# Half of the gate projections and the merge gate moved behind the scan, as pairs of column tiles computed with Strassen's seven block products

## The chip, the cores and the metric

The kernel runs on one core of one Trainium2 chip. The metric is device time in microseconds (us). The kernel before takes 2431.65 us, the median of three runs (2431.22 to 2434.09).

The engines are named as the profile names them: PE (TensorE matmul), PEld (its weight loads), DVE (VectorE), ACT (ScalarE), POOL (GpSimd) and SP (SyncE, which here issues every DMA, in the order of its queue). Each engine runs its own instructions in order. Semaphores join the engines.

## The reference, cut to what matters

Two layers of this are computed, over 1024 tokens of width 1024, in float32, and one final RMSNorm:

```python
h = rms_norm(x, norm_g) * (1.0 + scale) + shift
proj = h @ w_in                       # 1024 x 1024 times 1024 x 8320
pool_u, pool_g, q, k, v, ret_g, rw, rw_g, gate_logits = split(proj)
o_pool = causal_pool_mixer(pool_u) * silu(pool_g)
o_ret  = retention(q, k, v) * silu(ret_g)
o_rwkv = rwkv7_time_mix(rw) * silu(rw_g)      # a scan over the tokens
y = einsum('btnw,nwd->btnd', stack(o_pool, o_ret, o_rwkv), w_branch)
gates = sigmoid(gate_logits.reshape(B, T, 3, 1024))
x = x + gate * (sum(gates * y, axis=2) @ w_out)
```

The columns of `gate_logits` (24 tiles of 128, "gates" below) and of `rw_g` (4 tiles, "wg" below) depend on h alone and are needed only when the branches are merged. They can be computed at any time before that.

## The kernel before, in words

**Matmuls.** Everything is kept transposed: features on the 128 partitions, tokens along the free axis in two halves h of 512. A float32 value is split into two float32r parts (hi by a cast on ACT, lo by a subtraction on POOL or DVE: `split`, L561). A product of two such values is three matmuls: hi·hi, hi·lo, lo·hi (`mm1`, L548). One *item* is one 128-wide column tile of a weight matrix: for h @ w_in it is 2 halves of the tokens x 8 tiles of 128 features x 3 = 48 matmuls of 128x512 (`in_tile2`, L1431), which sum in two of the three PSUM buffers `acc` (L558). Its weights are loaded and split one item ahead by `wprep` (L512), through buffers `wr` (raw), `wh` and `wl` (hi, lo), three of each.

**The scan.** RWKV's scan is done in chunks of 64 tokens for four pairs of heads, one pair after the other (`rwkv_task`, L783). For each pair there is a preparation for either half of the tokens (`prepare`, L800: DVE and ACT work that makes AR, BK and Z; it begins with six `lw` matmuls), then transposes and scores (`scores`, L889: tiles bt, BKt, g, G), then the inversion of triangular blocks (`invert`, L928: 30 dependent steps `tm` on DVE; the matmuls `av`, then `m`), and then 16 chunk steps (L1004 to L1052), each a chain PE, DVE, PE, DVE, PE, DVE through the tiles two, xst, ch, Z, ch and S. After 8 steps comes a layer norm (L1055) and one transposition `yt` with the output `wob` (L1058).

**The order.** Independent chains (the lanes norm, post, rwkv, mix, ada; L310) are Python generators. Each yields how long it wants to wait by a cost model of its own; after every matmul of an item, `pump` (L415) advances the lanes that are due. So the matmuls of the items lie between the dependent matmuls of the scan and cover the time in which PE would wait. A scheduler in the tile layer then orders the instructions of each engine, and may pull an independent instruction forward. `plan_layer` (L471) decides which item comes next: the items of the next pair of heads (k, r, v), those of the retention of this pair (rq, rk, rv, rg) and of the pooling (pu, pg) when they may be used, and otherwise a gate ("pre") or, late, a wg ("late"). There is always an item to give. When the last pair of heads is nearly done, ("merge",) ends this stage; what is left of gates and wg follows, mixed with the branch projections `br`, and then the output projection `out`.

With this order 20 gates and 3 wg of the first layer and 16 gates and 3 wg of the second lie beside the scan; 4 and 8 gates and one wg each come after it. An early gate is stored to DRAM (`gd`, L1155) and loaded again for the merge (L1499). A wg is multiplied into the scan's output in DRAM (`od`: loaded, multiplied, stored; L1145 to L1150). `load_o` (L1471) loads these outputs for the branch projections through the four buffers `mo` and splits them (oz, oy, oG).

Of the kernel before, what the change touches and what calls it, by code (L numbers as in the profile page):

```python
# [9 lines left out]
F32 = mybir.dt.float32  # L10
# [7 lines left out]
P = 128  # L18
D = 1024
# [47 lines left out]
def GT(n, *ds):  # L67
    return [("gate", n, d) for d in ds]


def BR(n, *ds):
    return [("br", n, d) for d in ds]
# [17 lines left out]
for _c in (16, 20):  # L90
    ADA.append((_c, [_c + _i for _i in range(4)], _n))
    _n += 8
FIRST = [("lora",), ("k", 0), ("r", 0)]


@with_exitstack
def trunk_kernel(ctx, tc, xT, cvec, pos, vecs, consts, w_ada, w_all, pool_w, lora_w, out):
# [15 lines left out]
    def gtile(s):  # L113
        return gp.tile([P, 32 * P + 8], F32, tag="G", name=nm(s))
# [153 lines left out]
    def rope_tables():  # L268
        yield 15000
        MAGIC = 12582912.0  # L270
        TWO_PI = 2.0 * math.pi
        cw, left = [], TWO_PI
        for _ in range(3):
            e = 2.0 ** (math.frexp(left)[1] - 8)
            cw.append(math.floor(left / e) * e)
            left -= cw[-1]
        cw.append(left)
        PI_F = 3.1415925
        for h in range(2):
            s = slice(h * HF, (h + 1) * HF)  # L280
            pi = t_ri("posi", I32)
            tc.keep_in_program_order(nc.sync.dma_start(out=pi, in_=pos[:, s].to_broadcast([P, HF])))
            ang = t_ri("ang")
            nc.vector.tensor_copy(ang, pi)
            nc.vector.tensor_scalar_mul(ang, ang, cs("freq"))
            n = t_ri("nrot")
# [6 lines left out]
            m = t_ri("over")  # L293
# [103 lines left out]
    def until(t):  # L397
        return max(0.0, t - clock[0])
# [72 lines left out]
    def plan_layer(l):  # L471
        yield from [("lora",)] + RW(0)
        pools = deque(PL(i) for i in range(4))
        pre = deque(GT(0, *range(8)) + GT(1, 0, 1, 4, 5, 6, 7) + GT(2, 2, 3, 4, 5, 6, 7, 0, 1) + GT(1, 2, 3))
        late = deque([("wg", 0), ("wg", 1), ("wg", 2)])
        done = 0
        while done < 4 or prog.get((l, 3), 0) < 13 or pools or halves[l] < 15:
            if done < 4 and prog.get((l, done), -1) >= 0:
                done += 1
                if done < 4:  # L480
                    yield from RW(done)
                yield from RT(done - 1)
            elif pools and 4 - len(pools) <= done and len(lanes["mix"]) < 2:
                yield from pools.popleft()
            elif pre or late:
                q = late if late and (done == 4 and prog.get((l, 3), -1) >= 0 or not pre) else pre
                it = q.popleft()
                early[l].add(it)
                yield it
            elif pools:  # L490
                yield from pools.popleft()
            elif done < 4:
                done += 1
                if done < 4:
                    yield from RW(done)
                yield from RT(done - 1)
            else:
                break
        yield ("merge",)
        seq = GT(1, 2, 3) + BR(0, 0, 2, 4, 6) + [("wg", 0), ("wg", 1)]  # L500
        seq += GT(1, 0, 1) + BR(1, 0) + [("wg", 2), ("wg", 3)] + BR(1, 2) + GT(1, 4, 5) + BR(1, 4)
        seq += GT(1, 6, 7) + BR(1, 6)
        seq += GT(2, 0, 1) + BR(2, 0) + GT(2, 2, 3) + BR(2, 2) + GT(2, 4, 5, 6, 7) + BR(2, 4, 6)
        yield from [it for it in seq if it not in early[l]]
        for part in range(2 + (l + 1 == L)):
            yield from [("out", d, part) for d in out_order(l, part)]

# [2 lines left out]
    wready = deque()  # L510

    def wprep(big=False):  # L512
        for l, it in planner:
            if it != ("merge",):
                break
            wready.append((it, None))
        else:
# [128 lines left out]
    def affine_lo(x, r, eng):  # L646
        eng.tensor_tensor(r[1], x, r[0].bitcast(F32), op=ALU.subtract)
# [135 lines left out]
    def rwkv_task(l, hp, kT, rT, vp, lt, lw):  # L783
# [507 lines left out]
    with tc.manual_schedule(engines={ET.PE, ET.DVE, ET.Activation, ET.Pool}):  # L1291
# [114 lines left out]
        mms(1, 6)  # L1406
        mms(1, 7)
    seen[0] = len(nc.cur_bb.bb.instructions)
    L_ = (0, {}, {}, [])
    L_[3].extend(lora_load(0))  # L1410
    for i in range(3):
# [8 lines left out]
    for l in range(L):  # L1420
# [35 lines left out]
        while late_ada:  # L1456
            task = add("ada", ada(*late_ada.pop(0), t_lt))
            if len(gate_ada) < 2:
                gate_ada.append(task)
        merged = None  # L1460
        gates = {}

# [28 lines left out]
        def prefetch():  # L1491
            for j in range(min(2, len(brs))):
                n, d0 = brs[j]
                for d in (d0, d0 + 1):
                    if ("gate", n, d) in early[l] and (n, d, 0) not in gates:
# [220 lines left out]
```

## Time and profile before

| | |
|---|---|
| median of three runs | 2431.65 us |
| the profiled execution's own time | 2434.12 us |
| its span, first to last instruction | 2432.3 us |
| around the span | 1.8 us |
| mean granted clock of TensorE | 0.991 |
| DMA | 219.46 MB, mean 90 GB/s |

Read it by stage: up to about 80 us the first norm and the first three items; then, for each of four pairs of heads, some 200 us of preparation, inversion and chunk steps with items between them (first layer up to 914 us, second from 1263 to 2090 us); then what is left of the gates with the branches, and the output projection. Busy shares are averages over these stages.

### The profile page before, as it was taken

To read this page: it belongs to the slowest core of one execution; us is meant where nothing else is said; L and a number is where in the kernel's file an instruction comes from. 1 tells how busy PE (TensorE), PEld (TensorE's weight loads), DVE (VectorE), ACT (ScalarE), POOL (GpSimd) and SP (SyncE) were. 2 spreads that over 40 slices of the span, in tenths; PEclk is the share of its full clock that TensorE was granted. 3 is DMA by queue.
4 is the path that set the end of the run, shared out by engine and by line. 5 is a ranking of instruction groups with operands and counts; after the bars stand their busy time and mean duration, and the time that the engine had idled before them with its cause. 6 is when DMAs were issued, how large, how long until landed. Compare 5 with 4: busy or idle time off the path is not lost. (4 is left out here: it accounts for less than half of the span.)

```text
span 2432.3 us, 34706 instructions
## 1 busy us (share of the span) xinstructions
PE 2347.7 (97%) x13312; PEld 1921.0 (79%) x13312; DVE 1310.9 (54%) x2564; ACT 800.1 (33%) x1481; POOL 819.3 (34%) x729
## 2 busy tenths in 40 slices
PE   5989999999999999999999999999999999999998
PEld 4768878877877888877877887787788788788888
DVE  7664476467368642457455646836745764221344
ACT  5542242233333223122443324323323323312243
POOL 4321332233231424462442232323323332546241
PEclk9999999999999999999999999999999999999999
DMA  7132112111123225656431211211211222552242
GB/s 252 49 101 79 40 36 80 41 38 62 62 64 93 84 71 179 195 182 221 132 118 41 69 40 36 88 35 49 67 53 38 69 79 68 167 156 91 83 126 79
DMA packets 121910, 219.46 MB, mean 90 GB/s; under 512 B 13840, under 2 KB 17168, under 8 KB 121744
## 3 DMA queue, kind: packets, MB, share of 16 engines
q1 hardware_dynamic: 121744, 217.24, 28.7%
q8 instruction: 104, 1.70, 0.3%
q14 instruction: 62, 0.51, 0.1%
HBM read 172.36 MB, written 44.83 MB: 89 GB/s over the span
## 5 line engine op out<-in xcount | busy, mean ns | idle before, releaser
L563 POOL TENSOR_TENSOR wl<-wr,wh 128x512 fp32r<-128x512 f32 x342 | 456.0, 1334 | 1089.1 <-ACT wh L562 1004.1
L445 PE MATMUL acc<-hlo,wh 128*128 128x512 f32 x2000 | 807.7, 404 | 0.0
L445 PE MATMUL acc<-hhi,wh 128*128 128x512 f32 x2000 | 806.5, 403 | 0.0
L445 PE MATMUL acc<-hhi,wl 128*128 128x512 f32 x2000 | 804.5, 402 | 1.5 <-POOL r L1074 1.5
L445 PEld LDWEIGHTS acc<-hhi,wl 128*128 128x128 f32 x2000 | 378.4, 189 | 68.9 <-POOL r L1074 2.0
L445 PEld LDWEIGHTS acc<-hhi,wh 128*128 128x128 f32 x2000 | 378.4, 189 | 67.8 <-issue 1.1
L445 PEld LDWEIGHTS acc<-hlo,wh 128*128 128x128 f32 x2000 | 378.6, 189 | 67.2 <-issue 2.7
L562 ACT CAST wh<-wr 128x512 fp32r<-128x512 f32 x342 | 211.7, 619 | 654.3 <-PE acc L445 418.7
L1036 DVE SCALAR_TENSOR_TENSOR S<-ch,pc,SP 64x64 f32<-64x64 f32 x256 | 72.5, 283 | 107.6 <-PE ch L445 105.2
L1024 DVE TENSOR_TENSOR xst<-two,MT 64x128 f32<-64x128 f32 x128 | 37.6, 293 | 146.2 <-PE two L445 127.0
L1012 ACT ACTIVATE SP<-S,pc 128x128 f32<-128x128 f32 x128 | 51.4, 402 | 179.8 <-DVE S L1036 171.0
L1540 DVE SCALAR_TENSOR_TENSOR mrg<-gs,acc 128x512 f32<-128x512 f32 x32 | 21.9, 687 | 118.8 <-PE acc L445 118.7
L1542 DVE SCALAR_TENSOR_TENSOR gs<-gs,acc 128x512 f32<-128x512 f32 x64 | 43.6, 683 | 78.0 <-PE acc L445 76.0
L445 PE MATMUL acc<-oz,wh 128*128 128x512 f32 x256 | 81.3, 397 | 1.8 <-DVE gs L1542 1.5
L949 DVE TENSOR_TENSOR two<-two,tm 64x30 f32<-64x30 f32 (+14 forms) x240 | 79.0, 329 | 7.4
L445 PE MATMUL acc<-oy,wh 128*128 128x512 f32 x256 | 80.7, 395 | 1.2 <-DVE mrg L1540 0.8
L943 DVE TENSOR_TENSOR tm<-MT,two 64x30 f32<-64x30 f32 (+14 forms) x240 | 76.4, 318 | 8.2 <-ACT two L936 1.1
L445 PE MATMUL acc<-oG,wh 128*128 128x512 f32 x256 | 79.7, 393 | 0.6 <-DVE gs L1542 0.6
L1031 DVE COPY Z<-ch 64x128 f32<-64x128 f32 x128 | 36.0, 282 | 78.5 <-PE ch L445 77.9
L235 DVE SCALAR_TENSOR_TENSOR ada_acc<-wada,cact,ada_acc 128x512 f32<-128x512 f32 (+1 forms) x70 | 58.8, 840 | 31.5 <-DMA wada<-in_w_ada 30.7
L575 POOL TENSOR_TENSOR vr<-vr,fixed 128x8 f32<-128x8 f32 (+1 forms) x32 | 43.7, 1366 | 85.9 <-DVE vr L574 56.8
L445 PE MATMUL acc<-mhi,wh 128*128 128x512 f32 (+1 forms) x176 | 65.4, 371 | 0.7 <-DVE xres L1588 0.7
(298 smaller groups left out, 3899.6 us busy)
## 6 DMA issues: line engine op xcount, KB each, us to landing
wr<-in_w_all SPq DMA_DIRECT2D x364, 256.0 KB, 2.7
gd<-gsg SPq DMA_DIRECT2D x72, 256.0 KB, 2.0
gs<-gd SPq DMA_DIRECT2D x72, 256.0 KB, 3.4
wada<-in_w_ada SPq DMA_DIRECT2D x70, 256.0 KB, 2.9
ol<-od SPq DMA_DIRECT2D x64, 256.0 KB, 3.0
ringG<-in_w_ada SPq DMA_DIRECT2D x26, 256.0 KB, 4.9
x<-in_xT SPq DMA_DIRECT2D x16, 256.0 KB, 4.9
od<-po SPq DMA_DIRECT2D x16, 256.0 KB, 2.0
```

The lines of the kernel that those rows point to most:

```text
L235: nc.vector.scalar_tensor_tensor(part if kt < NKT - 1 else acc, w, cact[:, kt : kt + 1], part, op0=ALU.mult, op1=ALU.add)
L445: return nc.tensor.matmul(out, lhsT=lhsT, rhs=rhs, start=start, stop=stop, **kw)
L562: nc.scalar.copy(hi, src)
L563: eng.tensor_tensor(lo, src, hi.bitcast(F32), op=ALU.subtract)
L575: nc.gpsimd.tensor_tensor(x, x, mhalf.to_broadcast([P, x.free_size()]), op=ALU.pow)
L943: nc.vector.tensor_tensor(pr, L3[:, i + 1 :, i : i + 1].to_broadcast([64, n, i]), M3[:, i : i + 1, 0:i].to_broadcast([64, n, i]), op=ALU.mult,
L949: nc.vector.tensor_tensor(M3[:, i + 1 :, 0:i], M3[:, i + 1 :, 0:i], pr, op=ALU.add)
L1012: nc.scalar.activation(SP, S, AF.Copy, scale=pcc)
L1024: nc.vector.tensor_tensor(xst[0:64, :], cy[64:128, 0:P], AV[:, c * P : (c + 1) * P], op=ALU.add)
L1031: nc.vector.tensor_copy(Z[0:64, c, :], ch[0:64, 0:P])
L1036: nc.vector.scalar_tensor_tensor(Sn[rw, rw], ch[rw, P + 64 * hd : P + 64 * hd + 64], pc[rw, c : c + 1], SP[rw, rw], op0=ALU.mult, op1=ALU.add,
L1542: nc.vector.scalar_tensor_tensor(s, s, 1.0, ps, op0=ALU.add, op1=ALU.mult)
```

## The change

In each layer at most 12 of the 24 gates now lie beside the scan: `EARLY` caps their number at 4, 6, 8, 10 and 12 as pairs of heads get ready, and where no other item may be given either, the plan yields ("idle",): the planner moves its clock on to the next due lane and gives PE nothing. After the merge come two gates as before. The other ten gates and the four wg are seven pairs of column tiles. A pair is a product of 256 x 1024 weights with 1024 x 1024 activations: 2 x 2 blocks (each block of weights 128 columns x 512 features, each block of h 512 features x 512 tokens). It is computed by seven block products with sums taken before and after (Winograd's order of them) and not by eight. The branch projections then follow without a break.

For this, h is stored to DRAM when it is made (16 tiles of 256 KB per layer) and loaded again (16 tiles, `traw`); four combinations of its blocks are formed on DVE and split (`form`); for each pair of column tiles four weight tiles are loaded (`wraw`), four sums are formed on DVE and seven operands are split (`wforms`); a product is 12 matmuls (`prod`). Between the products ACT copies three partial sums and DVE adds two. Also, the first scores of a pair of heads now wait in the planner for Z, and the tables of the rotary positions are built in other buffers.

In the built program 7752 matmuls write 128x512 sums of items, 168 fewer than the 7920 before (7 pairs x 12 x 2 layers). DVE has 132, ACT 116, POOL 58 and SP 112 instructions more. 96 gate halves are stored to DRAM and loaded again, not 72.

```diff
+EARLY = (4, 6, 8, 10, 12)
...
     xd = [dp.tile([8, 2, P, HF], F32, name=f"xd{l}") for l in range(1)]
+    hd = [dp.tile([8, 2, P, HF], F32, name=f"hd{l}") for l in range(L)]
...
-        pre = deque(GT(0, *range(8)) + GT(1, 0, 1, 4, 5, 6, 7) + GT(2, 2, 3, 4, 5, 6, 7, 0, 1) + GT(1, 2, 3))
-        late = deque([("wg", 0), ("wg", 1), ("wg", 2)])
+        gates = deque(GT(0, *range(8)) + GT(1, *range(8)) + GT(2, *range(8)))
...
-            elif pre or late:
-                q = late if late and (done == 4 and prog.get((l, 3), -1) >= 0 or not pre) else pre
-                it = q.popleft()
-                early[l].add(it)
-                yield it
...
+            elif 24 - len(gates) < EARLY[done]:
+                yield gates.popleft()
             else:
-                break
+                yield ("idle",)
         yield ("merge",)
...
+        for _ in range(2 + len(gates) % 2):
+            yield gates.popleft()
+        rest = list(gates) + [("wg", i) for i in range(4)]
+        yield ("forms", [(rest[i], rest[i + 1]) for i in range(0, len(rest), 2)])
+        for n in range(3):
+            yield from BR(n, 0, 2, 4, 6)
...
+            nc.sync.dma_start(out=hd[l][kt, late], in_=xs[kt])
...
-            yield until(whole[h] + 1000)
+            yield max(until(whole[h] + 1000), wait(Z))
...
+            if ws is None:
+                clock[0] = max(clock[0], min((due[k] for k in names if lanes[k]), default=0.0))
+                pump()
+                wprep()
+                continue
...
+        def form(f, room):
+            sub = lambda o, x, y: nc.vector.tensor_tensor(o, x, y, op=ALU.subtract)
+            for kt in range(4):
+                b11, b12, b21, b22 = raws[4 * kt : 4 * kt + 4]
+                if f == 0:
+                    sub(b11, b12, b11)
+                elif f == 1:
+                    sub(b12, b22, b12)
+                    sub(b22, b22, b11)
+                elif f == 3:
+                    sub(b21, b21, b22)
+                x = (b11, b22, b12, b21)[f]
+                hi, lo = room(kt)
+                split(x, hi, lo, nc.vector if kt % 2 else nc.gpsimd)
+                TT[f].append((hi, lo))
+                yield 1300
...
+            for i in range(len(pairs)):
+                a11, a21, a22, a12 = nxt
+                yield wsplit(a11)
+                s1 = comb(a21, a22, ALU.add)
+                yield wsplit(s1)
+                s2 = comb(s1, a11, ALU.subtract)
+                yield wsplit(s2)
+                yield wsplit(a12)
+                yield wsplit(comb(a11, a21, ALU.subtract))
+                yield wsplit(comb(a12, s2, ALU.subtract))
+                if i + 1 < len(pairs):
+                    nxt = loads(i + 1)
+                yield wsplit(a22)
...
+        for p, (ia, ib) in enumerate(pairs):
+            last = p + 1 == len(pairs)
+            ca = acc_ps()
+            prod(ca, b11, True)
+            cd, cb = acc_ps(), acc_ps()
+            nc.scalar.copy(cb, ca)
...
+            prod(cd, TT[0], True)
+            s5 = t_cc("s5")
+            nc.scalar.copy(s5, cd)
...
+            prod(cb, TT[1], False)
+            s2 = t_cc("s2")
+            nc.scalar.copy(s2, cb)
+            prod(ca, b21, False)
+            evac(ia, ca, 0)
...
+            prod(cb, TT[2], False)
+            nc.vector.tensor_tensor(s5, cb, s5, op=ALU.add)
+            evac(ib, s5, 1)
+            prod(cd, b22, False)
+            nc.vector.tensor_tensor(s2, cd, s2, op=ALU.add)
+            evac(ia, s2, 1)
...
+            prod(cb, TT[3], False)
+            evac(ib, cb, 0)
```

More of the change, by code (lines that the diff above doesn't have):

```diff
@@ L292, in rope_tables @@
                 yield 6000
-            m = t_ri("over")
+            m = mi("over")
             nc.vector.tensor_scalar_add(n, ang, math.pi / 2)
@@ L512, in wprep @@
     def wprep(big=False):
+        if wready and wready[-1][0][0] == "forms":
+            return
         for l, it in planner:
-            if it != ("merge",):
+            if it[0] not in ("merge", "idle", "forms"):
                 break
             wready.append((it, None))
+            if it[0] != "merge":
+                return
         else:
@@ L1408, in trunk_kernel @@
     seen[0] = len(nc.cur_bb.bb.instructions)
+    for h in range(2):
+        for kt in range(8):
+            nc.sync.dma_start(out=hd[0][kt, h], in_=xin[h][kt])
     L_ = (0, {}, {}, [])
@@ L1459, in trunk_kernel, with load_h @@
                 gate_ada.append(task)
+        TT = [[] for _ in range(4)]
+        raws = []
+        def load_h(kt, tile_):
+            for k, h in ((kt, 0), (kt, 1), (kt + 4, 0), (kt + 4, 1)):
+                x = (next(tile_) if kt == 2 else tile_)("traw")
+                nc.sync.dma_start(out=x, in_=hd[l][k, h])
+                raws.append(x)
+        def form(f, room):
[14 more added lines that the diff above has]
+                yield 1300
@@ new lines, in trunk_kernel, with roomy, room @@
+        for kt in range(4):
+            load_h(kt, mi if kt < 2 else t_ri if kt == 3 else iter((t_vp, t_vp, t_cs, t_cs)))
+        def roomy(n):
+            t = []
+            def room(kt):
+                if n == 2:
+                    if kt == 0:
+                        t.append(gtile("T"))
+                    o = 2 * kt * HF
+                elif n < 2:
+                    if kt % 2 == 0:
+                        t.append(r8("T"))
+                    o = kt % 2 * D
+                else:
+                    return hb("thi"), hb("tlo")
+                return t[-1][:, o : o + HF].bitcast(F32R), t[-1][:, o + HF : o + D].bitcast(F32R)
+            return room
@@ new lines, in trunk_kernel, with loads @@
+        tasks = [add("norm", form(f, roomy(f))) for f in range(3)]
+        while wready[0][0][0] != "forms":
+            it, ws = wready.popleft()
+            wprep()
+            for h, ps in enumerate(in_tile2(ws)):
+                evac(it, ps, h)
+        pairs = wready.popleft()[0][1]
+        tasks.append(add("norm", form(3, roomy(3))))
+        drain("post")
+        def loads(i):
+            a, b = pairs[i]
+            r = []
+            for it, j in ((a, 0), (b, 0), (b, 1), (a, 1)):
+                r.append((mi if i % 2 else t_rk)("wraw"))
+                nc.sync.dma_start(out=r[-1], in_=w_all[l, ITEMS.index(it), j])
+            return r
@@ new lines, in trunk_kernel, with prod @@
+        ready_w = deque()
+        source = wforms()
+        def prod(ps, b, first):
+            while len(ready_w) < 3:
+                w = next(source, None)
+                if w is None:
+                    break
+                ready_w.append(w)
+            if len(ready_w) == 1:
+                wprep()
+            w = ready_w.popleft()
+            settle()
+            if not first:
+                clock[0] = max(clock[0], ready.get(ps.tensor.name, 0.0))
+            for k in range(4):
+                ks = slice(k * P, (k + 1) * P)
+                for j, (x, y) in enumerate(((w[0], b[k][0]), (w[0], b[k][1]), (w[1], b[k][0]))):
+                    mmul(ps, x[:, ks], y, start=first and k + j == 0, stop=k == 3 and j == 2, skip_group_check=True)
+                    pump()
@@ L1494, in prefetch @@
                 for d in (d0, d0 + 1):
-                    if ("gate", n, d) in early[l] and (n, d, 0) not in gates:
+                    if (n, d, 0) not in gates:
                         if j and len(gs_free) < 7:
```

39 lines of the change are left out of this document (24 added, 15 removed).

## The prediction, made before the run

> **What bounds the kernel now.** I read the page first, then the waits of PE, then windows by stage, then the timeline of one pair of heads. The page's first part and three of its groups:
>
> ```profile
> span 2432.3 us, 34706 instructions
> PE 2347.7 (97%) x13312; PEld 1921.0 (79%) x13312; DVE 1310.9 (54%) x2564; ACT 800.1 (33%) x1481; POOL 819.3 (34%) x729
> ...
> L563 POOL TENSOR_TENSOR wl<-wr,wh 128x512 fp32r<-128x512 f32 x342 | 456.0, 1334 | 1089.1 <-ACT wh L562 1004.1
> ...
> L562 ACT CAST wh<-wr 128x512 fp32r<-128x512 f32 x342 | 211.7, 619 | 654.3 <-PE acc L445 418.7
> ...
> ol<-od SPq DMA_DIRECT2D x64, 256.0 KB, 3.0
> ```
>
> PE is busy for 97% of the span and no other engine for more than 54%. By stage (us, busy time and count of PE, granted clock, DMA share, GB/s) it is the same: a pair of heads in the scan, the last pair of the first layer, and the stage behind it.
>
> ```profile
> 306.00:508.00 202.00, 197.07 (x1214) 0.99 0.17 51
> 707.00:914.00 207.00, 200.21 (x1249) 0.98 0.28 85
> 914.00:1145.00 231.00, 228.47 (x1034) 1.00 0.61 192
> ```
>
> PE works without a break beside the scan (197 of 202 us) and behind it (228 of 231). What it waits for is little (us in total, times, longest):
>
> ```profile
> PE bt L451 <- ACT Z L872: 10.1, 6, 3.1
> PE two L445 <- ACT aT L809: 7.5, 1, 7.5
> ...
> PE acc L445 <- DVE gs L1542: 2.5, 4, 1.5
> ```
>
> So the time is PE's work, and an edit is worth the matmuls that it takes away, less each new wait of PE. The question is how many new waits come: before, the gates were the cover of the scan.
>
> **Term 1, the matmuls taken away.** Dense 128x512 matmuls of items, the first and the last of nine that follow each other:
>
> ```profile
> 470.37 0.39 PE L445 MATMUL acc<-hhi,wl 128*128 128x512 f32 x1
> 472.19 0.40 PE L445 MATMUL acc<-hlo,wh 128*128 128x512 f32 x1
> ```
>
> Eight steps take 1.82 us: 0.2275 us from start to start (the busy time of one, 0.39 us, overlaps with the next). 168 fewer are 168 x 0.2275 = **-38.2 us**. All of it is on the path, since PE is.
>
> **Term 2, cover taken from the scan.** From the built order: beside the scan the items have 281 matmuls less in the first layer and 219 less in the second. If the scan can't go faster than before, they leave 500 x 0.2275 = 113.8 us of holes; if it can, none. So I need the floor of each stretch of the scan without cover. First the preparation of the second pair of heads (last `lw` to first `av`), and behind it the inversion, to the first `m`:
>
> ```profile
> 328.43 0.39 PE L445 MATMUL lw<-lt,lw 64*128 64x512 f32 x1
> 331.73 0.78 PE L451 MATMUL bt<-cst,BK 128*128 128x128 f32 x4 [2.25 <-ACT Z L872]
> 351.35 0.69 DVE L858 TENSOR_TENSOR BK<-aT,Lc 128x512 f32<-128x512 f32 x1
> ...
> 367.68 0.68 DVE L907 TENSOR_TENSOR G<-two,cst 128x512 f32<-128x512 f32 x1
> 370.58 0.62 PE L445 MATMUL av<-Z,G 64*64 64x64 f32 x7
> 406.19 2.07 DVE L952 STREAM_TRANSPOSE MT<-two 32x1024 f32<-32x1024 f32 x1
> 420.63 1.19 PE L445 MATMUL m<-MT,G 32*32 32x32 f32 x32
> ```
>
> BK is whole at 352.04, 23.6 us behind `lw`; G is whole only at 368.36, because PE has items between its transposes and scores. Without them that part is 8 transposes, 16 pairs of scores and four evictions of 0.68 us: I estimate 7 us from these rows, so the floor of the stretch is 30.6 us. It took 42.15. The order now has 59 item matmuls there, not 98 (8.9 us less), and some 3 us of small matmuls of the retention go into the chunk steps. PE's own work falls to about 27 us (42.15 - 3.3 of waits - 8.9 - 3): a wait of 3.6 us, as much as now. In the other pairs that lose cover here (third and fourth of the first layer, third and fourth of the second) 90 to 114 become 52 to 61; the same sum gives waits of 0 to 8 us. Over the five I take **+13 us** more than now; ends 0 and 40.
>
> The inversion took 50.05 us from `av` to `m`, but T13 was there at 408.26: floor 37.7 us. The order takes 30 matmuls (6.8 us) and some small ones away: about 40 us of PE. No new wait.
>
> One chunk step:
>
> ```profile
> 473.86 0.38 PE L445 MATMUL two<-S,AR 128*128 128x128 f32 x2
> 474.35 0.29 DVE L1024 TENSOR_TENSOR xst<-two,MT 64x128 f32<-64x128 f32 x1 [0.93 <-PE two L445]
> 475.00 0.39 PE L445 MATMUL ch<-xst,G 128*65 128x64 f32 x4
> 475.44 0.28 DVE L1031 COPY Z<-ch 64x128 f32<-64x128 f32 x1 [0.79 <-PE ch L445]
> 476.22 0.38 PE L445 MATMUL ch<-Z,BKt 128*128 128x128 f32 x2
> 476.64 0.58 DVE L1036 SCALAR_TENSOR_TENSOR S<-ch,pc,SP 64x64 f32<-64x64 f32 x2 [0.92 <-PE ch L445]
> ```
>
> From a PE start to DVE's start are 0.49, 0.44 and 0.42 us, DVE's work is 0.29, 0.28 and 0.58, and each way back about 0.06: a floor of 2.7 us. Twelve item matmuls (2.73 us) and the step's own hide that with room. The order keeps 12 in most steps, but 9 in the last pair of each layer (2.05 us and some 0.7 of its own): at the floor, and there the scheduler has put subtractions of `form` (0.69 us each, as the BK row) among DVE's steps. With the stretch from `m` to the first step, where 36 become 5 in the first layer and 21 in the second, I take 8 us per last pair, **+16 us**; ends 0 and 40.
>
> **Term 3, from the scan to the products.** The last chunk step of the first layer, and the layer norm behind it:
>
> ```profile
> 913.75 0.40 PE L445 MATMUL two<-Z,G 128*65 128x64 f32 x4
> ...
> 921.51 1.04 POOL L709 TENSOR_TENSOR yc<-yc,vr 128x512 f32<-128x512 f32 x1
> ```
>
> 8.8 us pass until yc can be transposed. Now 47 matmuls lie between in the second layer; then 13 and 15 (3.0 to 3.4 us) stand ahead of `yt` in PE's queue, and the products behind it: a wait of 5 us. DVE then has wob, one subtraction and one sum (0.7 us each) ahead of the second product's weights, which need a cast (0.62) and a subtraction on POOL (1.33): 3 us more. **+16 us** in two layers; ends 4 and 24.
>
> **Term 4, from the products to the branches.** The last product ends with a wg. Its way from the sum to DRAM, as it is now:
>
> ```profile
> 921.86 0.60 ACT L1116 ACTIVATE wsg<-acc 128x512 f32<-128x512 f32 x1 [4.33 <-DMA od<-ol]
> 922.49 0.69 DVE L1117 SCALAR_TENSOR_TENSOR wsg<-wsg,acc 128x512 f32<-128x512 f32 x1 [0.77 <-ACT wsg L1116]
> 923.22 0.75 DVE L1149 SCALAR_TENSOR_TENSOR ol<-ol,vec,wsg 128x512 f32<-128x512 f32 x1
> ...
> 924.00 0.32 SPq L1150 DMA_DIRECT2D od<-ol  x1
> ```
>
> 2.2 us. In the new order this store stands on SP ahead of three of the four loads that the first branch matmuls need, so these wait behind the last product. One load lands after 3.0 us, a cast takes 0.62, and POOL's four subtractions 1.33 each: the last operand is there about 10.7 us behind the last product, and PE has 24 matmuls (5.5 us) to do with the first three. A wait of 8 us where nothing else lies between, **+16 us** in two layers; ends 0 and 24.
>
> **Term 5, the clock.** The stall of 2.25 us ahead of `bt`, the stretch behind it, and the same in the last pair (PE busy, granted clock):
>
> ```profile
> 329.00:332.00 3.00, 0.75 (x4) 1.00 0.01 3
> 332.00:335.50 3.50, 3.50 (x13) 0.52 0.00 0
> 335.50:340.00 4.50, 4.50 (x33) 1.00 0.25 62
> ...
> 728.00:735.00 7.00, 6.08 (x21) 0.51 0.62 187
> ```
>
> After such a stall PE runs at half clock for 3.4 to 6.8 us and so loses another 1.7 to 3.4. Terms 2 to 4 hold some nine stalls of over 2 us (three preparations, four of term 3, two of term 4): 9 x 1.7 = **+15 us**; ends 0 and 40. The Trainium skill (TensorE: Matmul & The Clock Gate, Part 1) has the clock fall only after an idle window of about 3.4 us; by that rule only the four long stalls of terms 3 and 4 count, +7 and not +15. The trace disagrees in the size of the gap: 2.25 us were enough.
>
> **Term 6, what runs denser.** In a pair POOL splits seven operands, 7 x 1.33 = 9.3 us, beside 84 x 0.2275 = 19.1 us of PE; ACT makes seven casts, three copies and four evacuations of some 0.6 us, 8.7; DVE six sums of 0.69 and its share of the adaLN work. They hide beside PE; without that cover POOL's part is 1.33 us of each product. The branches follow without gates between them; their wait now is 2.5 us (DVE gs). I take +4 us for both; ends 0 and 25. The 64 DMAs for h and 48 for gates are issued by SP beside the scan, at a DMA share of 0.17 to 0.28, and at 0.61 behind it: nothing, with one end in what they would delay (in the 25). The new wait for Z, ahead of `bt`, may save the 10.1 us of that row and moves what is queued behind `bt` on PE; I take nothing, ends -15 and 0.
>
> **Sum** against the profiled execution's own 2434.1 us (span 2432.3 and 1.8 around it): -38.2 + 13 + 16 + 16 + 16 + 15 + 4 = +41.8, 2475.9 us. That execution is 2.5 us above the median of the runs (2431.65), so the forecast for the median is **2474 us**.
>
> **The rivals.**
> - *The scan closes up and the edges are covered* (faster). The scheduler has pulled later items, forms and loads forward already; if the five preparations wait no more than now and the two edges cost half, the new waits come to some 17 us with little half clock, -38 + 17: 2411 us. It decides when terms 2 to 6 stay under 38.2 us. For it: `m` stood 12.4 us behind T13, so the scan has slack. Against it: DVE's 23.6 us to BK.
> - *The holes stay* (slower by much). The scan keeps its length since its order is the planner's and DVE's chain the bound: -38.2 + 113.8 + 47 (terms 3 to 5) = +123, 2554 us. Against it: floors of 30.6, 37.7 and 2.7 us against 42.15, 50.05 and some 3.9 now.
> - *The short stalls don't touch the clock.* Only the four longest (5 us in term 3, 8 us in term 4) cost a half clock of 1.7 us each, 7 us and not 15: 2465 us. For it: over a whole pair of heads, with its waits, the mean clock is still 0.99; against it the window at 332. This is what the rule of the Trainium skill (TensorE: Matmul & The Clock Gate) would make of it.
> - *It cancels*: waits of about 38 us, within 5 us of the time before.
>
> **How the numbers follow.** The forecast has 0.40, the clock rival 0.15, the holes 0.15, other slower mixtures of the ends 0.06; faster 0.18; no difference 0.06. A measurement of this kernel can tell about 0.2% (5 us) from no change: faster 0.18, same 0.06, slower 0.76. The range must reach into the first two rivals to leave no more than 2 in 10 out: 2408 to 2550 us. Among the slower cases alone the forecast's own range is 2450 to 2505.
>
> **What would show it.** Term 1: 168 item matmuls fewer at the same 0.228 us, and windows in the products in which PE is busy throughout. Term 2: gaps of PE ahead of `bt`, `g` and `av` in the preparations, released by DVE BK or G; a pair of heads that takes about 180 us, not 200, is the scan closing up. Term 3: PE yt waiting for yc, then a product waiting for POOL wl. Term 4: PE acc waiting for oz behind the last product. Term 5: more windows at a clock of 0.5. I am wrong if pairs of heads still take 200 us with long gaps, if the products wait for their weights, or if the edges show no gap.

## The result, and the profile after

The changed kernel takes **2487.41 us** (median of four runs, 2484.20 to 2492.41), the kernel before on the same chip 2432.87 us: ratio 1.0224, 95% interval 1.0203 to 1.0245, slower. The forecast was 2474 us. The profiled execution took 2484.2 us, its span 2482.4, at a mean granted clock of 0.974 (before 0.991).

The first lines of the changed kernel's page:

```profile
span 2482.4 us, 35126 instructions
PE 2348.1 (95%) x13144; PEld 1914.6 (77%) x13144; DVE 1433.0 (58%) x2696; ACT 866.1 (35%) x1597; POOL 913.0 (37%) x787
```

PE has 168 matmuls less and the same busy time, 2348.1 against 2347.7 us. So 38 us of work went away and the rest of PE's work became as much longer; the idle time came on top.

Where it happened is seen best in windows by stage (us, PE's busy time and count, granted clock, DMA share, GB/s): the scan and what lies behind it, for both layers. Before:

```profile
92.00:913.00 821.00, 795.37 (x4869) 0.99 0.21 65
913.00:1291.00 378.00, 373.22 (x1694) 1.00 0.53 166
1291.00:2090.00 799.00, 779.78 (x4836) 1.00 0.19 58
2090.00:2426.00 336.00, 333.17 (x1663) 1.00 0.38 116
```

After:

```profile
92.00:867.50 775.50, 742.84 (x4620) 0.98 0.21 65
867.50:1318.00 450.50, 425.83 (x1861) 0.97 0.55 174
1318.00:2083.50 765.50, 742.24 (x4619) 0.98 0.18 57
2083.50:2476.00 392.50, 372.14 (x1799) 0.97 0.43 139
```

Both scans together went from 1620 to 1541 us, 79 less; the 500 matmuls taken out of them are 113.8 us, so 35 us were lost there. Behind the scans it went from 714 to 843, 129 more; the 332 matmuls that came there on balance are 75.5 us, so 53 were lost. PE's idle time (length less busy) rose by 11 us in the scans (44.9 to 55.9) and by 37 behind them (7.6 to 45.0). The clock went from 0.99 and 1.00 to 0.97 and 0.98 everywhere: in the trace's record of it PE worked 34.4 us at half clock before and 97.0 after. In these stretches dense 128x512 matmuls start every 0.43 us (four steps from 886.33 to 888.04) and not every 0.2275, so about half of that time is lost, by estimate 17.2 against 48.5 us. The balance: -38.2 of matmuls, +50 of idle time, +31 of half clock, +43; the span grew by 50.1. About 7 us of slower work I can't place; by the same sums it lies in the scans, where of the 35 us lost 11 are idle time, 14 are half clock (PE worked 24.4 us at it there before, 51.7 after) and 10 are left.

The pairs of heads did close up. The second and the last pair of the first layer, and the products behind it:

```profile
311.00:499.00 188.00, 182.10 (x1169) 1.00 0.15 47
682.00:867.50 185.50, 171.78 (x1070) 0.94 0.33 104
867.50:1042.00 174.50, 152.48 (x662) 0.93 0.60 191
```

188 and 185.5 us stand against 202 and 207 before. In the second layer the third and the last pair went from 200 and 215 us to 194 and 185. PE is idle for 22 us of the 174.5 in the products. What PE waits for in the changed kernel (us, times, longest):

```profile
PE yt L453 <- POOL yc L706: 20.7, 4, 8.5
...
PE acc L447 <- ACT oz L558: 12.9, 2, 6.9
PE acc L447 <- ACT gsg L1151: 9.5, 3, 4.8
PE bt L453 <- ACT Z L869: 9.0, 5, 4.1
...
PE acc L447 <- DVE s L1601: 4.4, 3, 2.1
```

`yt` is the edge from the scan to the products, `oz` the edge from the products to the branches: both stops were forecast, and both are there in both layers. The rows behind the first one (start, us, engine, operation, the idle time before it):

```profile
866.31 2.99 POOL L559 TENSOR_TENSOR T<-traw,T 128x512 fp32r<-128x512 f32 x2 [0.41 <-ACT T L558]
...
869.40 3.45 POOL L559 TENSOR_TENSOR T<-traw,T 128x512 fp32r<-128x512 f32 x2
...
869.88 1.27 DVE L693 TENSOR_SCALAR mn<-mn 128x8 f32<-128x8 f32 x1
...
872.82 1.04 POOL L696 TENSOR_TENSOR yc<-y,mn 128x512 f32<-128x512 f32 x1
...
873.82 2.48 POOL L559 TENSOR_TENSOR T<-traw,T 128x512 fp32r<-128x512 f32 x2
...
875.27 1.06 DVE L570 TENSOR_SCALAR vr<-vr 128x8 f32<-128x8 f32 x1
876.41 1.63 POOL L571 TENSOR_TENSOR vr<-vr,fixed 128x8 f32<-128x8 f32 x1
878.12 1.04 POOL L706 TENSOR_TENSOR yc<-yc,vr 128x512 f32<-128x512 f32 x1
879.21 0.72 PEld L453 LDWEIGHTS yt<-cst,yc 128*128 128x128 f32 x4 [8.89 <-POOL yc L706]
```

POOL splits the T operands of the products ahead of, and in the middle of, the layer norm: between y and yc it has four splits in its queue, and so the way from the last chunk step to yc takes 11.8 us (867.32 to 879.16), not the 8.8 of before. 1.7 us of it are yc's wait in POOL's queue: mn is done at 871.15 and yc begins at 872.82. Two small operations on DVE, `mn` and `vr`, are slow besides: they take 1.27 and 1.06 us and took 0.17 each in the kernel before:

```profile
915.20 0.17 DVE L696 TENSOR_SCALAR mn<-mn 128x8 f32<-128x8 f32 x1
...
919.54 0.17 DVE L574 TENSOR_SCALAR vr<-vr 128x8 f32<-128x8 f32 x1
```

`vr` begins while POOL splits and ends with the split (876.33 and 876.30); at the second layer's edge it takes 1.06 us again and ends at 2092.34, the split at 2092.31. That POOL's splits hold DVE here is inferred from these ends; no run varied it.

### The profile page after: what moved, and what is told of

Read it like the earlier page. It is cut to its first block, busy times and chain, and to the rows that moved or that the text cites. A ratio compares the mean times of both kernels' runs of the same rounds, so it can differ in the third digit from the quotient of the medians.

```text
span 2482.4 us, 35126 instructions
## 1 busy us (share of the span) xinstructions
PE 2348.1 (95%) x13144; PEld 1914.6 (77%) x13144; DVE 1433.0 (58%) x2696; ACT 866.1 (35%) x1597; POOL 913.0 (37%) x787
## 5 line engine op out<-in xcount | busy, mean ns | idle before, releaser
L559 POOL TENSOR_TENSOR wl<-wr,wh 128x512 fp32r<-128x512 f32 x282 | 377.4, 1339 | 866.2 <-ACT wh L558 821.7
L447 PE MATMUL acc<-hhi,wh 128*128 128x512 f32 x1688 | 684.5, 405 | 10.4 <-ACT gsg L1151 9.5
L447 PE MATMUL acc<-hhi,wl 128*128 128x512 f32 x1688 | 686.2, 406 | 0.0
L447 PE MATMUL acc<-hlo,wh 128*128 128x512 f32 x1688 | 683.5, 405 | 0.0
L447 PEld LDWEIGHTS acc<-hhi,wh 128*128 128x128 f32 x1688 | 321.0, 190 | 69.9 <-ACT gsg L1151 10.9
L447 PEld LDWEIGHTS acc<-hlo,wh 128*128 128x128 f32 x1688 | 321.0, 190 | 58.0 <-issue 2.2
L447 PEld LDWEIGHTS acc<-hhi,wl 128*128 128x128 f32 x1688 | 321.0, 190 | 55.3 <-issue 0.7
L559 POOL TENSOR_TENSOR wl<-wsum,wh 128x512 fp32r<-128x512 f32 x56 | 78.6, 1405 | 114.2 <-ACT wh L558 111.2
L447 PE MATMUL acc<-T,wh 128*128 128x512 f32 x336 | 111.7, 415 | 2.7 <-ACT wh L558 2.7
L447 PE MATMUL acc<-oz,wh 128*128 128x512 f32 x256 | 85.3, 415 | 14.1 <-ACT oz L558 12.9
L447 PEld LDWEIGHTS acc<-T,wh 128*128 128x128 f32 x336 | 66.6, 200 | 18.1 <-ACT wh L558 3.1
```

The source lines that it names most:

```text
L447: return nc.tensor.matmul(out, lhsT=lhsT, rhs=rhs, start=start, stop=stop, **kw)
L559: eng.tensor_tensor(lo, src, hi.bitcast(F32), op=ALU.subtract)
```

## The experiments

Medians in us; before, on the same chips, was 2432.56 to 2433.3. All compute the whole reference; e4 adds matmuls that nobody reads.

| run | what it is | median | ratio (95%) |
|---|---|---|---|
| changed kernel | cap 4 to 12, 14 pairs | 2487.41 | 1.0224 (1.0203 to 1.0245) |
| e1_plain | cap 4 to 12, no pairs | 2484.05 | 1.0212 (1.0197 to 1.0227) |
| e2_wg_earlier | pairs, wg in the middle | 2491.87 | 1.0242 (1.0219 to 1.0265) |
| e3_two_more | 12 pairs, four gates ahead | 2478.84 | 1.0193 (1.0174 to 1.0213) |
| e4_keep_busy | pairs, unread matmuls at the edges | 2489.64 | 1.0225 (1.0205 to 1.0246) |
| e5_plain_cap22 | cap 22, no pairs | 2456.48 | 1.0096 (1.0081 to 1.0111) |
| e6_pairs_cap22 | cap 22, 5 pairs | 2461.80 | 1.0124 (1.0107 to 1.0142) |
| e7_pairs_mid | cap 6 to 17, 8 pairs | 2466.83 | 1.0143 (1.0115 to 1.0170) |
| e8_plain_o_first | e5, branch operands early | 2441.00 | 1.0033 (1.0023 to 1.0042) |
| e9_both_edges | changed kernel, both edges moved | 2463.43 | 1.0123 (1.0108 to 1.0139) |
| e10_mid_edges | e7, both edges moved | 2443.80 | 1.0043 (1.0027 to 1.0060) |
| e11_mid_cover | e10, more cover in layer 0 | 2440.34 | 1.0026 (1.0015 to 1.0038) |
| e12_high_edges | cap 6 to 19, 6 pairs, both edges moved | 2439.55 | 1.0030 (1.0019 to 1.0040) |

My theory was that of the prediction (each cover taken away and each edge brings a stop, and the stops bring half clock, so the sum eats the 38 us); the rival was that one of these, or the products by themselves, is all of it.

**e1, the pairs as plain items in the same place.**

```diff
-        yield ("forms", [(rest[i], rest[i + 1]) for i in range(0, len(rest), 2)])
+        yield ("forms", [])
+        yield from rest
```

(The stores and loads of h and the forms go with it.)

> Changes against the changed kernel: the seven pairs behind the scan are computed as fourteen plain items (168 matmuls more), h is not stored, loaded or combined. My theory (the seven products save PE work where they stand; the loss is waits at the edges and beside the scan, with half clock behind them): 168 x 0.2275 = 38 us more, less some 8 to 15 us of waits for the combinations of h and for the sums of the weights: 2510 to 2520 us. Rival (the products wait for their sums, splits and copies and so are the loss): no slower than the changed kernel's 2487, down to 2450.

It took 2484.05, not 2510 to 2520: the products are worth nothing here, although they take 168 matmuls away. Its windows behind the scans, and its two edges:

```profile
866.00:1313.00 447.00, 437.15 (x1951) 0.99 0.52 163
2078.00:2475.00 397.00, 388.35 (x1887) 0.99 0.42 134
```

```profile
PE yt L453 <- POOL yc L706: 10.2, 4, 3.6
...
PE acc L447 <- ACT oz L559: 5.9, 2, 3.3
```

447 + 397 us against 450.5 + 392.5: the same length with 38.2 us more of work. It is idle for 18.5 us there, the changed kernel for 45.0: 26.5 of the 38.2 are PE's new waits; the other 12 are slower work, at a clock of 0.97 and not 0.99 (PE worked 35.6 us at half clock there against e1's 14.7, which is 10 of the 12). The stops at `yt` and `oz` are each half as long or less without the products. So the whole 51 us that e1 has over before come from what is not Strassen: the cap, the new order and the small edits that come with them.

The products themselves run at full rate when nothing is in their way. Four pairs in a row of the changed kernel, each from its second product's first matmul to the next pair's:

```profile
932.04:953.70 21.66, 20.43 (x94) 1.00 0.66 220
953.70:978.20 24.50, 21.45 (x103) 1.00 0.59 177
978.20:999.87 21.67, 21.67 (x94) 0.92 0.64 208
999.87:1019.19 19.32, 19.32 (x86) 1.00 0.23 78
```

A pair is 84 matmuls; the others in these windows are small ones of the adaLN (8, 16, 8 and none). The last is 84 x 0.2275 = 19.1 us and a little. The third loses 1.7 us to half clock; the first two stop for a sum on DVE, for 1.23 and 2.06 us. The first of these stops:

```profile
942.57 3.48 DVE L236 SCALAR_TENSOR_TENSOR ada_acc<-wada,cact,ada_acc 128x512 f32<-128x512 f32 x2
...
946.08 0.49 DVE L234 TENSOR_SCALAR ada_acc<-wada,cact 128x512 f32<-128x512 f32 x1
946.49 0.68 DVE L1601 TENSOR_TENSOR s<-acc,s 128x512 f32<-128x512 f32 x1
...
947.32 0.47 PE L447 MATMUL acc<-thi,wh 128*128 128x512 f32 x1 [1.23 <-DVE s L1601]
```

The sum s must have read the accumulator before the seventh product writes on into it, and it stands in DVE's queue behind the adaLN's work. A plain item has no such wait: nobody reads its bank until it is whole.

**e2, the wg pairs in the middle of the seven**, so that their stores don't stand on SP ahead of the branch operands' loads.

```diff
-        rest = list(gates) + [("wg", i) for i in range(4)]
+        rest = list(gates)
+        rest[6:6] = [("wg", i) for i in range(4)]
```

> Only the order of the pairs: the two pairs of wg come after the third pair, and two pairs of gates are last. My theory (SP holds the loads of the branch operands behind the last wg's store, 6.0 and 6.9 us of PE, and half clock for 6.8 and 10.2 us behind it): both gaps go, and some 5.7 us of half clock with them: 15 to 19 us less, about 2470. Rival (those loads are late for another reason, the buffers or POOL's splits): the gaps stay above 3 us and the time within 5 us of 2487.

2491.87, no gain, and the waits of PE still hold this line:

```profile
PE acc L447 <- ACT oz L559: 9.9, 2, 5.0
```

The stop shrinks by 1 to 2 us an edge and stays. A wg store ahead of the loads is at most 3 of the 12.9 us. The rows of the changed kernel tell the rest:

```profile
1036.85 0.38 SPq L1625 DMA_DIRECT2D ol<-od  x1
...
1039.04 0.32 SPq L1147 DMA_DIRECT2D od<-ol  x1
1039.41 4.55 SPq L1625 DMA_DIRECT2D ol<-od  x4
...
1041.18 0.62 ACT L558 CAST oz<-ol 128x512 fp32r<-128x512 f32 x1 [4.08 <-DMA ol<-od]
```

The first load of a branch operand is issued at 1036.85, 1.4 us after the last product's last matmul began (1035.49). All of the preparation begins when the products are over. And the stop ends at 1041.85 with the first operand, whose load stands ahead of the wg's store (1039.04).

**e3, four gates after the merge in place of two, and one pair less per layer.**

```diff
-        for _ in range(2 + len(gates) % 2):
+        for _ in range(4 + len(gates) % 2):
```

> Four gates instead of two come plainly behind the merge, and one pair fewer per layer is done by products (24 matmuls more, +5.5 us). My theory (yt waits 8.5 and 8.0 us for the layer norm since PE has 13 to 15 matmuls to do; half clock for 17.1 and 13.7 us behind it): the wait falls to 5 us or less as 2 more evacuations' worth of matmuls come first, and the half clock behind it goes: 10 to 20 us less net, 2467 to 2477. Rival (the products' first operands are late whatever stands ahead): the wait moves behind yt, and the time is 2487 to 2495.

2478.84, just above the range and 8.6 below the changed kernel. The stops at `yt` are still 7.4 and 6.3 us, since the tile layer's scheduler moves the transposes forward again, to 23 and 24 matmuls of items behind the scan: most of the new cover came after them.

**e4, matmuls that nobody reads: 32 ahead of `yt`, 24 ahead of the first branch.** It adds 112 matmuls, 25.5 us of PE at full rate, to see what stops and clock cost when PE is kept at work.

```diff
+        dummy(32)
         drain("post")
...
+        dummy(24)
         merged = None
```

> Adds matmuls whose result nobody reads at the two edges of each layer: 32 between the scan and yt, 24 between the last product and the first branch matmul (7.3 and 5.5 us of PE). They fill the waits and shorten none. Theory (the half clock follows from PE's waiting): the half-clock stretches at the four edges (17.1, 6.8, 13.7 and 10.2 us with 29 us of work in them) go, 10 to 14 us less although 112 matmuls are added: about 2475. Rival (the clock falls there for another reason, or the waits are not what bounds the edges): the added 25.5 us are paid in part or whole, 2487 to 2512.

2489.64, so not what I expected of the clock: it lies in the rival's range, near its lower end. PE's work at half clock fell from 97.0 to 73.9 us (11.5 won by the same estimate) and the stops at `oz` went, but the stops at `yt` stayed at 6.0 each. There the run doesn't do what it was meant to: in the trace only 23 and 21 of the 32 matmuls come ahead of `yt`, and the other 9 and 11 behind it. 25.5 us of useless work for +2 us of time says that most of it lay in time that was lost anyway; it doesn't part idle time from clock. I count it as undecided on the clock.

**e5, e6 and e7, the cap.** e5 is e1 with `EARLY = (22,) * 5`; e6 and e7 are the changed kernel with

```diff
-EARLY = (4, 6, 8, 10, 12)
+EARLY = (22,) * 5              # e6
+EARLY = (6, 9, 12, 15, 17)     # e7
```

> All items plain, no Strassen pairs, no h store or reload; the changed kernel's plan with the cap on early gates lifted to 22 of 24, so that the scan's four stages of a layer hold about as many 128x512 matmuls as in the kernel before (626, 627, 603 and 615, 607, 619 between scans, against 625, 592, 612 and 604, 626, 639). Theory A (the 51 us that the all-plain version with the cap lost are a matter of place: work taken out of the scan where it had cover and put behind it where it has none, with the stops and the half clock that this brings): 2425 to 2445 us, about the kernel before. Rival B (what the plan has besides, the scores' wait for Z's bank, looking one item ahead instead of four, costs time by itself): 2455 us or more, with stops of TensorE of the same sum as under the cap (87.7 us).

> The changed kernel with the cap lifted to 22: three pairs in layer 0 and two in layer 1 are left for the block products, 60 matmuls (13.7 us) fewer than the run above of the same cap. Theory A (the products pay their steady rate, and what they lose is one preparation and two edges per layer, whatever the number of pairs): the preparations and edges eat more than 13.7 us, so 0 to 20 us over the run above. Rival C (each pair loses by itself what it saves): the same time as the run above, within 4 us, or less.

> The changed kernel with the cap at 6, 9, 12, 15 and 17 gates in place of 4, 6, 8, 10 and 12: four pairs per layer, 96 matmuls (21.8 us) fewer than all-plain. If the loss of the change is in proportion to the gates that the cap takes out of the scan (24 gates beside it cost 51 us in the all-plain version), half as many moved cost about 25 us, and with the products' sum near zero the time is 2445 to 2465 us. If the cap costs nothing and the edges everything, it stays at 2480 or more.

e5 took 2456.48, which is rival B's time, at its lower edge. Lifting the cap brings back 27.6 of the 51 us, so my theory was half of it; 23 us over before stay, and e8 shows that most of them have another cause than rival B named. e6 is 5.3 us above e5 with 60 matmuls (13.7 us) fewer, as theory A had it: 19 us lost for five pairs. e7, halfway, is at 2466.83, 2 us above its range.

**e8, where the other 23 us of e5 were.** By its windows all of it lies behind the scan, where the branches now follow each other with no gates between, and begin to prepare operands only then. e8 is e5 with this moved up, ahead of the plain items:

```diff
+        for nh in ((0, 0), (0, 1), (1, 0)):
+            next_o(*nh)
         while wready[0][0][0] != "br":
```

> All-plain with the cap at 22 as before (2456.5 us, 23 over the kernel before, all of it behind the scan: last ch to the end 393 + 348 us against 378 + 336), and the first three preparations of branch operands (od's loads and splits) are begun ahead of the plain items behind the merge gate, not behind them, as in the kernel before. Theory A (the branch edge costs because its operands begin too late): the stops at the first branches (2.9, 3.6, 2.4 and 3.3 us for oz, oG and oy) go, 2440 to 2448 us. Rival B (twelve branch items in a row, without gates between them, are the cost: VectorE and the gate loads fall behind): 2452 us or more, with the stops moved into the branches.

2441.00, as theory A said. Its windows behind the scan:

```profile
917.40:1301.00 383.60, 371.86 (x1687) 1.00 0.55 173
2093.40:2432.60 339.20, 337.81 (x1685) 1.00 0.46 143
```

383.6 + 339.2 against 393.2 + 347.9 in e5. The start of the operands was worth 15.5 us in the median. 8 us over before are left; twelve branches in a row without gates, the scores' wait for Z and the shorter look ahead (rival B of e5) are still different, and none of them was tried by itself.

**e9 and e10, both edges moved in the kernel with products**: the operands of the first branches are begun ahead of the last pair, and the last `yt` comes behind the whole first pair (in e9 pinned in the program's order; e10 to e12 have no pin, and `yt` comes 67 and 124 matmuls of items behind the scan in e10). e10 has the cap of e7.

```diff
         for p, (ia, ib) in enumerate(pairs):
             last = p + 1 == len(pairs)
+            if last:
+                next_o(0, 0)
+                next_o(0, 1)
...
             evac(ib, cb, 0)
+            if p == 0:
+                go[l] = 1
+                drain("post")
```

> The changed kernel with the same work and cap, and two things moved: the last yt transposes of each layer come behind the whole first pair (85 and 87 matmuls behind the scan's last two, before 13 and 15), and the first two branch operands are begun ahead of the last pair instead of behind it. Theory A (the edges cost what they show: 8.5 + 8.0 us at yt, 6.0 + 6.9 us at oz, and some 10 us of half clock around them): 2487 - 30 to 2487 - 40, so 2447 to 2460 us. Rival B (the stops only move, to the forms and preparations of the first pair or to VectorE in the branches): 2470 us or more.

> The changed kernel with the cap at 6, 9, 12, 15, 17 (four pairs per layer) and both edges moved as in the run with the changed kernel's cap (yt 67 and 124 matmuls behind the scan). The same cap with the edges in their old place gave 2466.8 us, with 14.1 us of stops at yt and 9.4 us at oz. Theory A: 2435 to 2447 us, about the kernel before. Rival B: 2455 or more.

e9: 2463.43, 24 us less and between the two. The stops at `oz` are gone. Those at `yt` are gone too, and this stands in their place among PE's waits:

```profile
PE acc L447 <- ACT wh L559: 14.1, 2, 7.7
PE acc L447 <- POOL wl L560: 9.9, 10, 2.8
```

The second product now waits for the high half of its weights, 7.7 and 6.4 us, and then 2.8 and 2.4 for the low half. The first of these waits is for a sum of weights on DVE (`wsum`, at 875.89 and 2079.59), and it stands in DVE's queue right behind the layer norm's `vr` (875.82 and 2078.62). So moving `yt` away from PE left the layer norm ahead of the operands on DVE. e10 took 2443.80, in the range of theory A: with more plain matmuls ahead of the pairs (layer 1) there is no stop at this edge at all. In layer 0 PE stops for 5.3 and 3.9 us ahead of products that read T, but what it waits for there is an accumulator that isn't emptied yet:

```profile
PE acc L447 <- ACT gsg L1154: 10.1, 2, 5.3
...
PE acc L447 <- DVE wsg L1117: 3.9, 1, 3.9
```

The `gsg` that ends the first stop stands on ACT behind casts that wait for DVE; the `wsg` of the second stands on DVE behind the adaLN's work and that of the wg before it.

**e11 and e12, can it beat the kernel before?** e11 has four plain gates ahead of layer 0's pairs, e12 two and a higher cap with three pairs per layer.

```diff
-        for _ in range(2 + len(gates) % 2):
+        for _ in range(2 + 2 * (l == 0) + len(gates) % 2):   # e11
-EARLY = (6, 9, 12, 15, 17)
+EARLY = (6, 10, 14, 17, 19)                                  # e12
```

> The run with the middle cap and both edges moved (2443.8 us), with four plain gates in place of two ahead of the pairs in layer 0: one pair fewer there (12 matmuls, 2.7 us, more), and 24 plain items' matmuls more over which the T halves can be made. In that run layer 0 stopped 5.3 and 3.9 us for T, with 6.8 us of half clock beside it, and layer 1, which had more plain matmuls ahead of its pairs, not at all. Theory A (a preparation is free once enough plain work is ahead of it): the two stops go, 2443.8 + 2.7 - 9 - 3, so 2432 to 2438 us. Rival B (the split halves are late because VectorE and GpSimd are busy with the post's work and the raw loads, however long the cover): 2442 us or more.

> Both edges moved, the cap at 6, 10, 14, 17, 19 and three pairs per layer: 72 matmuls (16.4 us) fewer than the all-plain run with cap 22 and the operands begun early (2441 us), 24 more than with four pairs (2443.8). If the products pay where they are covered, as theory A has it: 2441 - 16 + 5 to 10 for preparations, so 2428 to 2437 us, the kernel before or a little better. Rival C (whatever is saved in products goes into preparations and waits, pair by pair): 2441 us or more.

2440.34 and 2439.55: neither, and both between what the two theories said. In e11 the first of e10's two stops (5.3 us) went and 3.0 of the second are left. The first, which came of the operands' casts, went with more plain work ahead, as theory A had it; the second is DVE's `wsg` and not T, as the expectation had it. e12 has 72 matmuls (16.4 us) fewer than e8 and is 1.5 us below it: rival C nearer than theory A. Their caps differ, so this isn't a clean price of a product; but in all three comparisons (this one, the changed kernel against e1, e6 against e5) the saved matmuls don't come out as time.

## Why the prediction was right, and where it was off

The sign was right, and so was the size roughly: +41.8 by its sum, +50.1 in the span, +54.5 between the medians. That the size came out is in part luck: the terms for waits (2, 3, 4 and 6) came to 65 us and PE's idle time grew by 50, the clock was put at 15 and took 31, and the two errors cancel. The steps:

- **Term 1** (-38.2): right as a count and a price, since an undisturbed pair takes 19.32 us.
- **Term 2** (+29, cover taken from the scan): the scans lost 35 us, but not as I said. I looked for gaps ahead of `bt` and `av`. PE waits 9.0 us at `bt` for Z, before 10.1; all idle time of the scans grew by 11 us. Another 14 are half clock, which I had put into term 5, and 10 are slower work without a known cause. The rival with the holes fell: the scans are 79 us shorter, not as long as before.
- **Term 3** (+16): the size is right, 8.5 + 8.0 us at `yt`. The step that failed is the sum of 5 for the layer norm and 3 for the weights: the splits of T on POOL, which I had left out there, make the layer norm late, and the wait for the weights behind it was only 0.3 us in the first layer (2.7 and 0.6 in the second). e9 shows that with `yt` out of the way about the same time is spent waiting for weights behind the same layer norm.
- **Term 4** (+16): the size is right (6.0 + 0.6 and 6.9), and the cause that I gave, the wg's store ahead of the loads on SP, fell with e2. Its sum didn't give its size either: the last operand at 10.7 us, less 5.5 us of matmuls, is a wait of 5.2 and not of 8. The wait is for the first operand: the loads begin when the products have ended. e8 and e9 began them earlier, and the stops went.
- **Term 5** (+15): mis-sized; 31 us were lost. I priced nine stalls of over 2 us with one slow window each. The number was right: the changed kernel's trace has 18 stretches at half clock and that of before 9, nine more. Their length was not: behind the edges they are 6.8 to 17.1 us long, in the scans up to 13.7, and they hold 62.6 us more of PE's work, not nine times 3.4. Short stalls are enough, which the clock rival denied, and the clock can stay down while PE works. Windows of the changed kernel around a stop of 2.37 us ahead of `bt` in the third pair of the first layer (PE's busy time, granted clock):

```profile
525.30:528.00 2.70, 0.34 (x3) 1.00 0.34 97
528.00:532.00 4.00, 4.00 (x15) 0.57 0.00 0
```

The same of e1 in the third pair of the second layer, where the cap has thinned the items out:

```profile
1745.00:1749.60 4.60, 3.11 (x18) 1.00 0.33 120
1749.60:1773.50 23.90, 23.25 (x119) 0.50 0.09 33
1773.50:1777.00 3.50, 3.50 (x19) 1.00 0.00 0
```

The second line is 23.9 us at half clock with PE at work for 23.25. The changed kernel has 13.7 us of half clock in the same place, the kernel before none. So taking cover away cost twice here: the stop, and a clock that came back late.

- **Term 6** (+4): 4.4 us of waits for `s` behind DVE's adaLN work; no run parts the rest of it from the other terms. The edits that I put at nothing (64 DMAs for h and 48 for gates on SP, the wait for Z) show no stop of their own.

The rival that came nearest the truth on what could be had is the first, with covered edges: e10 to e12 cover them and arrive at 2440 to 2444, 0.3 to 0.4% over before, not at 2411. What I had not seen in it is that also the products' saving needs cover that the scan no longer lends.

What stays open: the 8 us that e8 has over before, whether the half clock by itself costs what I put down to it (e4 can't tell), the 7 us of slower work without a place, and the clean price of a product with all its operands ready.

## What to carry to other kernels

Where one engine is busy for 97% of the time, as here, its independent work covers the dependent chains beside it: before work is moved out of such a stretch, price the stretch it leaves and the two edges of the stretch it goes to, and begin the next stage's loads and splits while the last one still runs. A faster algorithm with fewer matmuls but more dependent sums and splits pays only as far as those have cover too; here 168 matmuls fewer gave nothing. Test such a change in two parts, the new order with the old arithmetic first (e1): it showed at once that 51 us were lost without any product.

## What the runs showed of the hardware that I had not expected

The half clock came in windows of about 3.4 us or multiples of it. In the changed kernel 14 of its 18 stretches began in or right behind a stop of 1.7 us or more. But not each such stop brought one: stops of 2.15, 2.33 and 2.45 us (at 336, 1718 and 2060 us) left the clock at 1.00, while e1 fell to half clock for 3.4 us behind the stops of 2.31 and 2.08 us that answer to the last two. And ahead of the 23.9 us above, which are seven such windows in a row with PE at work, no stop of e1 in the 7 us before was longer than 1.2 us. The Trainium skill (TensorE: Matmul & The Clock Gate, Part 1) has the clock return after at least one busy window of about 3.4 us. That stretch disagrees with a return after the first: PE was busy throughout its last six windows, and the clock stayed at 0.50. Which matmuls were in it (by groups of e1's lines, instances and mean ns):

```profile
L447 PE MATMUL av<-Z,G 64*64 64x64 f32 x62 | 7.6, 312 | 0.0
L447 PE MATMUL g<-AR,BK 64*128 64x128 f32 x16 | 3.8, 427 | 0.0
...
L447 PE MATMUL acc<-hhi,wl 128*128 128x512 f32 x5 | 3.5, 694 | 0.0
```

Most were small ones on half of the array's rows, with 15 wide ones of items between; the kernel before has 79 wide ones in the 28 us around its `av` of the same pair, and no half clock there. That the small ones are the reason is argued, not shown: no run varied them alone.
